# The order of VectorE, ScalarE, GpSimd and the transfers from the scheduler's other model

## The chip, the cores and the metric

The kernel runs on one core of a Trainium2 chip. The metric is device time in microseconds (us), from the start of the program on the core to its end. A core has five engines that run their own instruction queues side by side: TensorE (PE, matrix products), VectorE (DVE), ScalarE (ACT), GpSimd (POOL) and SyncE (SP, which here only issues transfers). An instruction starts when its engine has done the ones before it in its queue and when the operands and buffers that it waits for are ready. The order within a queue is fixed when the program is built.

## The reference

One layer of a hybrid diffusion block, on 512 latent tokens (x) and 256 context tokens (ctx), 2048 wide, all in float32. The core of it:

```python
mod = silu(c) @ w_ada + b_ada
shift, scale, gate = split(mod, 3)             # and the same for ctx, from c_ctx
h  = rms_norm(x, norm_w) * (1 + scale) + shift
hc = rms_norm(ctx, norm_w) * (1 + scale_c) + shift_c
qkv_g, z_g, gates, q_a, k_a, v_a, z_a = split_proj(h @ w_in)       # hc likewise

q, k, v = silu(centred_conv(qkv_g, conv_w))    # 5 taps; q and k are then l2-normed per head
beta = sigmoid(gates[0]); g = -exp(a_log) * softplus(gates[1] + dt_bias)
# 8 heads, two directions, chunks of 64 tokens, first ctx, then latent:
#   v_new = u - w @ s;  o = (q * exp(g)) @ s + intra @ v_new
#   s     = s * exp(g_last) + (k * exp(g_last - g)).T @ v_new
gdn = rms_norm(o_forward + o_backward) * silu(z_g)

attn = softmax(rope(norm(q_a)) @ rope(norm(k_a)).T / sqrt(128)) @ v_a * silu(z_a)   # 8 heads, 2 kv heads
y = concat(gdn, attn) @ w_out
out = rms_norm(x + gate * y, final_norm_w)
```

## The kernel before

The float32 products are made of three passes: each operand is split into a high part (`whi`, `hhL`) and a low part (`wlo`, `hL`), and PE adds high by high, high by low and low by high (L146 to L148 `mm3`, L164 `one`). For each weight piece SP loads the raw tile (`wraw`), ACT casts the high part (L129), and DVE or POOL subtracts the low part (L130); three buffers each go round.

The stages, in time:

- **Start and first projection** (0 to 158 us). Six tiles of 1 MB (`xs`, L296) bring ctx and x; `turn` transposes them on PE. `ada` multiplies c by w_ada, eight groups of four tiles (`wada0_0` is group 0, tile 0; L352 loads, L355 multiplies). From a group's sums (L364) `make_h` builds h for two slices of 128 channels (`hhL` L399, `hL` L401), and `project` (L422) adds their share of the k, q and v columns of the first two heads (`klat`, `qlat`, `vlat`). `first_weights` (L381, L138) loads those columns (`wraw_w0`, `w0r`), L484 the gate columns (`wg`), L503 to L505 constants (`ctri`, `adt`).
- **Gates and the first head** (158 to 215 us). `gates(0, 1)` evaluates the gate formula of head 0 and `gates(1, 8)` that of heads 1 to 7, a chain of 16 small instructions on DVE each (L530 to L540, 128x12 and 128x84). PE sums them up along the tokens (`gcp` L547, L551), DVE copies `gcum` (L552) and `gts` (L564), and two transfers bring the sums back spread over partitions (`growd` L565, then `gr` L631, in the profile `grh`). `conv` (L204) makes the convolution of k, q and v of a head: ACT the first product (L217), DVE the other four taps (L221), ACT an exponential (L224, L225), DVE the last product into `kq`, `kc`, `vv` (L237). `gdn_prep(h)` transposes q and k on PE (`t1`, `t2`, `t3`, L640 to L653), builds the decay matrix in `gr` (L681, L684 on DVE, the exponential L686 on ACT), multiplies (`gq` L693, `IB`, `gr` L240, L702, L709), and inverts. Zero fills (L229) of `ktok`, `IB` and `UU` are ACT's.
- **Scan** (215 to 850 us). `gdn_scan(h)` takes eight heads in turn, twelve steps each. A step is a chain over three engines: `ks` (PE, L852 to L857), `rh` (DVE, L866), `ts` (PE, L875), `vs` and `vn` (ACT, L879, L882), `tsh` (PE, L886), `sth` (DVE, L892); POOL scales the old state (`sdh`, L240). Between these PE runs projections of later heads as filler; meanwhile DVE and ACT prepare the next head.
- **Attention** (850 to 1113 us), eight heads with the z projections as filler.
- **Output projection and end** (1113 to 1303 us). `out_block` (L1497) multiplies by w_out in four blocks of 512 columns; in the first, `merged` (L1486) splits the sixteen input tiles on the way (`mh` on ACT L1491, `ml` on DVE L1492). Each block's `epilogue` (L1522) adds x (`yx`, loaded at L1535) and squares; the last block keeps its weights (`rawl`, L1546). Then the norm and the stores.

**What sets the order.** The code is traced under a `TileContext`. When the context closes, its scheduler orders each engine's queue, among instructions whose inputs it takes to be ready, by the order in the code, moved forward by `tc.high_priority(offset=...)` (so `first_of_all`, offset 2500, round `rh`, `vs` and `sth` of the scan and round the gates of head 0). Two stretches are exempt (`tc.manual_schedule`): there an engine's queue is the order in which the code is written. For PE that is all from L283 to the end of attention; for ACT, DVE and POOL it is the attention. What the scheduler orders is therefore ACT, DVE and POOL outside attention, SP everywhere, and PE in the output projection.

## Time and profile before

| | us |
|---|---|
| median of the runs (lowest 1305.47, highest 1527.16) | 1306.19 |
| the profiled execution | 1304.42 |
| its span | 1302.6 |
| PE busy | 1250.4 |
| DVE busy | 842.5 |
| ACT busy | 583.4 |
| POOL busy | 141.9 |

The profiled execution is one run of the program; its span is the time between the first and the last instruction that the profiler recorded, 1.8 us less than the time of that execution. A row of a timeline gives start and duration in us, engine, line, operation, output and inputs; in brackets, how long the engine had stood idle before it and what ended that. "DVE rh L866" there means that the engine waited for the instruction of L866 on DVE which writes `rh`.

### The profile page before, as it was taken

The numbers are of one execution on the slowest core, as the hardware profiler recorded it, in microseconds if no ns is written. First come the engines' busy times: TensorE is split into PE (matmuls) and PEld (weight loads), VectorE is DVE, ScalarE is ACT, GpSimd is POOL, SyncE is SP. The second block draws the span as 40 slices with busy tenths as digits, with TensorE's granted clock in tenths as the row PEclk, the third lists the DMA queues.
The fourth block names the chain that finished last, engine by engine and source line by source line (L and its number), as shares of the span: only waits on it lengthen the run. The fifth ranks groups of instructions, "written<-read, shape, count | busy, mean of one in ns | idle before, by whom it ended". The sixth has DMA issues, their size and how long they took to land. (4 is left out here: it accounts for less than half of the span.)

```text
span 1302.6 us, 24348 instructions
## 1 busy us (share of the span) xinstructions
PE 1250.4 (96%) x9226; PEld 1018.4 (78%) x9226; DVE 842.5 (65%) x1893; ACT 583.4 (45%) x1464; POOL 141.9 (11%) x206
## 2 busy tenths in 40 slices
PE   6799999999999999999999999999999999999997
PEld 4466688888888888888888877787888888788885
DVE  5444596686867678675776646537888887555432
ACT  4222363455545454544545444535555444434211
POOL 1323100111111111111111001100000000000000
PEclk9999999999999999999999999999999999999998
DMA  9999424231332313222132443356443443475302
GB/s 354 316 326 347 133 67 107 60 67 55 74 72 62 78 47 83 67 69 57 54 83 75 106 131 110 99 164 214 149 129 114 123 140 102 161 244 190 93 33 97
DMA packets 227000, 164.53 MB, mean 126 GB/s; under 512 B 62210, under 2 KB 198491, under 8 KB 225859
## 3 DMA queue, kind: packets, MB, share of 16 engines
q1 hardware_dynamic: 226586, 162.87, 42.9%
q8 instruction: 73, 1.20, 0.4%
q14 instruction: 44, 0.36, 0.1%
q10 hardware_dynamic: 297, 0.11, 0.0%
HBM read 148.85 MB, written 14.08 MB: 125 GB/s over the span
## 5 line engine op out<-in xcount | busy, mean ns | idle before, releaser
L240 POOL TENSOR_TENSOR sdh<-sth,egl 128x256 f32<-128x256 f32 x80 | 56.9, 711 | 446.6 <-DVE sth L892 344.8
L871 ACT ACTIVATE oqh<-ksh,egsw 64x128 f32<-64x128 f32 x128 | 46.3, 362 | 92.7 <-DVE rh L866 86.4
L866 DVE SCALAR_TENSOR_TENSOR rh<-ksh,negeg,vtokh 64x128 f32<-64x128 f32 x176 | 61.2, 348 | 31.1 <-PE ksh L854 24.5
L146 PE MATMUL po<-whi_wo,mh 128*128 128x512 f32 x192 | 76.2, 397 | 0.0
L148 PE MATMUL po<-whi_wo,ml 128*128 128x512 f32 x192 | 76.1, 396 | 0.0
L147 PE MATMUL po<-wlo_wo,mh 128*128 128x512 f32 x192 | 76.1, 396 | 0.0
L1361 PE MATMUL zl<-hhL,whi_z 128*128 128x512 f32 x176 | 74.0, 421 | 0.0
L1361 PE MATMUL zl<-hhL,wlo_z 128*128 128x512 f32 x176 | 69.8, 396 | 0.0
L1361 PE MATMUL zl<-hL,whi_z 128*128 128x512 f32 x176 | 69.6, 395 | 0.0
L130 DVE TENSOR_TENSOR wlo_wo<-wraw_wo,whi_wo 128x512 fp32r<-128x512 f32 x48 | 33.0, 690 | 55.5 <-ACT whi_wo L129 55.3
L886 PE MATMUL tsh<-vsh,ktok 128*128 128x128 f32 x352 | 56.6, 283 | 6.7 <-ACT vnh L882 3.5
L886 PEld LDWEIGHTS tsh<-vsh,ktok 128*128 128x128 f32 x352 | 47.4, 190 | 16.0 <-ACT vnh L882 7.9
L129 ACT CAST whi_wo<-wraw_wo 128x512 fp32r<-128x512 f32 x48 | 29.6, 620 | 67.3 <-PE po L148 56.8
L892 DVE TENSOR_TENSOR sth<-sdh,tsh 128x256 f32<-128x256 f32 x80 | 33.6, 420 | 27.4 <-PE tsh L886 19.2
L879 ACT ACTIVATE vsh<-tsh,cch 128x128 f32<-128x128 f32 x88 | 32.2, 366 | 38.4 <-PE tsh L875 37.1
L164 PE MATMUL vl<-hhL,wlo_v 128*128 128x512 f32 x112 | 46.3, 413 | 0.0
L164 PE MATMUL vl<-hhL,whi_v 128*128 128x512 f32 x112 | 46.2, 413 | 0.0
L164 PE MATMUL vl<-hL,whi_v 128*128 128x512 f32 x112 | 45.8, 409 | 0.0
L1402 DVE SCALAR_TENSOR_TENSOR gacc<-graw,scol,gacc 128x512 f32<-128x512 f32 x60 | 44.9, 748 | 1.0
L950 ACT CAST pth<-pt 128x512 fp32r<-128x512 f32 x48 | 26.8, 585 | 40.7 <-PE pt L1289 40.7
L146 PEld LDWEIGHTS po<-whi_wo,mh 128*128 128x128 f32 x192 | 36.2, 188 | 9.5 <-ACT whi_wo L129 0.8
L148 PEld LDWEIGHTS po<-whi_wo,ml 128*128 128x128 f32 x192 | 36.2, 189 | 8.7
(540 smaller groups left out, 3890.2 us busy)
## 6 DMA issues: line engine op xcount, KB each, us to landing
wada<-in_w_ada SPq DMA_DIRECT2D x64, 512.0 KB, 8.6
graw<-in_w_ada SPq DMA_DIRECT2D x64, 256.0 KB, 3.1
wraw_wo<-in_w_out SPq DMA_DIRECT2D x48, 256.0 KB, 3.3
wraw_z<-in_w_in SPq DMA_DIRECT2D x44, 256.0 KB, 3.1
wraw_v<-in_w_in SPq DMA_DIRECT2D x28, 256.0 KB, 2.9
wraw_k<-in_w_in SPq DMA_DIRECT2D x24, 256.0 KB, 2.9
wraw_q<-in_w_in SPq DMA_DIRECT2D x24, 256.0 KB, 2.8
xs<-in_x SPq DMA_DIRECT2D x4, 1024.0 KB, 5.4
```

What stands on the lines that cost most here:

```text
L130: (lo_eng or G).tensor_tensor(out=lo, in0=raw, in1=hi, op=ALU.subtract)
L146: T.matmul(out, lhsT=lh, rhs=rh, start=start, stop=False, skip_group_check=True)
L147: T.matmul(out, lhsT=lh, rhs=rl, start=False, stop=False, skip_group_check=True)
L148: T.matmul(out, lhsT=ll, rhs=rh, start=False, stop=stop, skip_group_check=True)
L164: T.matmul(out, lhsT=lw, rhs=rt[m], start=k == 0 and n == 0, stop=k == KT - 1 and n == 2, skip_group_check=True)
L240: eng.tensor_tensor(out=out, in0=x, in1=y, op=ALU.mult)
L866: V.scalar_tensor_tensor(out=r[rows], in0=ks[rows, d], scalar=gsc["negeg"][rows, gcol:gcol + 1], in1=vtok[rows, p], op0=ALU.mult, op1=ALU.add)
L871: S.activation(oq[rows, v, p - 2], ks[rows, d], AF.Copy, scale=gsc["egsw"][rows, gcol:gcol + 1])
L886: T.matmul(ts[:, d], lhsT=ktok[:, p, half], rhs=vs, start=True, stop=True, skip_group_check=True)
L892: V.tensor_tensor(out=sn, in0=sd, in1=ts[:, 0:2], op=ALU.add)
L1361: T.matmul(pl, lhsT=lw, rhs=rt, start=k == 0 and m == 0, stop=k == KT - 1 and m == 2, skip_group_check=True)
L1402: V.scalar_tensor_tensor(out=acc, in0=raw, scalar=scol[:, k:k + 1], in1=acc, op0=ALU.mult, op1=ALU.add)
```

## The change

The `TileContext` is told to schedule with its other model. Without the argument it orders by priority with a simple model of readiness; with it, it follows a simulated time line of the engines and picks, for each engine, from what that time line has ready. The instructions are the same ones; PE up to the output projection and the other engines in the attention keep their order.

```diff
@@ -1586,7 +1586,7 @@
         arrays[f"in_{name}"] = arr
         aps[name] = nc.dram_tensor(f"in_{name}", arr.shape, mybir.dt.from_np(arr.dtype), kind="ExternalInput").ap()
     aps["out"] = nc.dram_tensor("out_y", (1, SEQ, D), F32, kind="ExternalOutput").ap()
-    with tile.TileContext(nc) as tc:
+    with tile.TileContext(nc, schedule_with_timeline_sim=True) as tc:
         build(tc, aps)
     r = run_bass_kernel_spmd(nc, [arrays], core_ids=[0])
     return r.results[0]["out_y"]
```

The order changes in hundreds of places; three are shown.

SP, right behind the six loads of `xs`, before (`wada0_0` to `wada0_3` are the first group of w_ada, two transfers each; `wraw_w0_k` and `w0rk` the first projection's weights of slice k; `wg` the gate columns):

```order
L352 DMA wada0_0_372<-in_w_ada 128x4x256 x2
L352 DMA wada0_1_379<-in_w_ada 128x4x256 x2
L352 DMA wada0_2_426<-in_w_ada 128x4x256 x2
L352 DMA wada0_3_433<-in_w_ada 128x4x256 x2
L138 DMA wraw_w0_0_451<-in_w_in 128x2x256
L381 DMA w0r0_457<-in_w_in 128x128
L138 DMA wraw_w0_1_463<-in_w_in 128x2x256
L381 DMA w0r1_469<-in_w_in 128x128
L484 DMA wg_153<-in_w_in 128x16x32
L138 DMA wraw_w0_2_499<-in_w_in 128x2x256
L381 DMA w0r2_505<-in_w_in 128x128
```

And now, from `wraw_w0_2` on; ahead of it stand, in the same sequence as before, `wraw_w0_0`, `w0r0`, `wraw_w0_1`, `w0r1` and `wg` (`ctri` and `adt` are constants of the gates, `nd2` two areas in memory that are cleared from the zeroed `UU0`):

```order
L138 DMA wraw_w0_2_499<-in_w_in 128x2x256
L352 DMA wada0_0_372<-in_w_ada 128x4x256 x2
L381 DMA w0r2_505<-in_w_in 128x128
L503 DMA ctri_110<-in_ctri 128x512
L504 DMA adt_158<-in_a_log 128x16
L505 DMA adt_158<-in_dt_bias 128x16
L352 DMA wada0_1_379<-in_w_ada 128x4x256 x2
L1047 DMA nd20_1634<-UU0_105 48x1024
L1047 DMA nd21_1635<-UU0_105 48x1024
L352 DMA wada0_2_426<-in_w_ada 128x4x256 x2
L138 DMA wraw_w0_3_551<-in_w_in 128x2x256
L352 DMA wada0_3_433<-in_w_ada 128x4x256 x2
```

The first group of w_ada moved behind the weights of three slices, the gate columns, the constants and the two clearings; its last tile also behind the weight of a fourth.

DVE, at the convolution of q of head 0, before (`cacc_q0` are the four taps, `kq0` q's product, `ug` and `gg` the gate formula; 128x12 is head 0, 128x84 heads 1 to 7):

```order
L221 SCALAR_TENSOR_TENSOR cacc_q0_1601<-craw2_1554,cvT_78,cacc_q0_1601 128x512
L130 TENSOR_TENSOR wlo_q0a_0_1836<-wraw_q0a_0_1833,whi_q0a_0_1835 128x512
L221 SCALAR_TENSOR_TENSOR cacc_q0_1601<-craw2_1554,cvT_78,cacc_q0_1601 128x512
L552 COPY gcum_84<-gcp_0_1743 128x12
L221 SCALAR_TENSOR_TENSOR cacc_q0_1601<-craw2_1554,cvT_78,cacc_q0_1601 128x512
L559 TENSOR_SCALAR negeg_85<-negeg_85 128x12
L534 TENSOR_SCALAR ug_112<-w_g_115 128x84
L221 SCALAR_TENSOR_TENSOR cacc_q0_1601<-craw2_1554,cvT_78,cacc_q0_1601 128x512
L564 COPY gts__117<-gtr_0_1767 12x128
L130 TENSOR_TENSOR wlo_q0a_1_1880<-wraw_q0a_1_1877,whi_q0a_1_1879 128x512
L237 SCALAR_TENSOR_TENSOR kq0_1583<-craw2_1554,cacc_q0_1601 128x4x64 x2
L536 SCALAR_TENSOR_TENSOR ug_112<-ug_112,w_g_115 128x84 x5
```

And now (`grh0` is the decay matrix of head 0, which comes from the `gr` load):

```order
L564 COPY gts__117<-gtr_0_1767 12x128
L237 SCALAR_TENSOR_TENSOR kq0_1583<-craw1_1553,cacc_k0_1585 128x4x64 x2
L130 TENSOR_TENSOR wlo_q0a_1_1880<-wraw_q0a_1_1877,whi_q0a_1_1879 128x512
L237 SCALAR_TENSOR_TENSOR kc0_1584<-craw1_1553,cacc_k0_1585 128x2x64 x2
L221 SCALAR_TENSOR_TENSOR cacc_q0_1601<-craw2_1554,cvT_78,cacc_q0_1601 128x512 x2
L681 TENSOR_TENSOR grh0_1785<-grh0_1785,gcum_84 128x768
L221 SCALAR_TENSOR_TENSOR cacc_q0_1601<-craw2_1554,cvT_78,cacc_q0_1601 128x512
L684 TENSOR_TENSOR grh0_1785<-grh0_1785,cmain_75 128x384 x2
L221 SCALAR_TENSOR_TENSOR cacc_q0_1601<-craw2_1554,cvT_78,cacc_q0_1601 128x512
L237 SCALAR_TENSOR_TENSOR kq0_1583<-craw2_1554,cacc_q0_1601 128x4x64 x2
```

`L681` and `L684` moved in between the taps. The 128x84 instructions, here in part before and gone now, moved ahead of the taps of k, one behind each of 128x12; these rows stand there now, just before the first tap of k (`cacc_k0`):

```order
L538 TENSOR_SCALAR ug_112<-ug_112 128x12
L538 TENSOR_SCALAR ug_112<-ug_112 128x84
L539 SCALAR_TENSOR_TENSOR zg_111<-zg_111,ug_112 128x12
L539 SCALAR_TENSOR_TENSOR zg_111<-zg_111,ug_112 128x84
L540 SCALAR_TENSOR_TENSOR gg__116<-zg_111,ag_113 128x12
L540 SCALAR_TENSOR_TENSOR gg__116<-zg_111,ag_113 128x84
L221 SCALAR_TENSOR_TENSOR cacc_k0_1585<-craw1_1553,cvT_78,cacc_k0_1585 128x512
L221 SCALAR_TENSOR_TENSOR cacc_k0_1585<-craw1_1553,cvT_78,cacc_k0_1585 128x256
```

Each instruction of head 0's chain is now followed by the same one for seven heads, and the taps of k follow both; before, they stood one by one between the 128x12 rows.

DVE, in the scan of head 1 while head 3's k is convolved and head 2 is prepared, before (`sth1_2` is the state after step 2 of head 1, `rh1_3` the first product of step 3):

```order
L130 TENSOR_TENSOR wlo_q3_2_3781<-wraw_q3_2_3778,whi_q3_2_3780 128x512
L221 SCALAR_TENSOR_TENSOR cacc_k3_3627<-craw2_1554,cvT_78,cacc_k3_3627 128x512
L221 SCALAR_TENSOR_TENSOR cacc_k3_3627<-craw2_1554,cvT_78,cacc_k3_3627 128x256
L221 SCALAR_TENSOR_TENSOR cacc_k3_3627<-craw2_1554,cvT_78,cacc_k3_3627 128x512
L892 TENSOR_TENSOR sth1_2_3687<-sdh1_2_3611,tsh1_2_3651 128x256
L221 SCALAR_TENSOR_TENSOR cacc_k3_3627<-craw2_1554,cvT_78,cacc_k3_3627 128x512
L221 SCALAR_TENSOR_TENSOR cacc_k3_3627<-craw2_1554,cvT_78,cacc_k3_3627 128x256
L221 SCALAR_TENSOR_TENSOR cacc_k3_3627<-craw2_1554,cvT_78,cacc_k3_3627 128x512
L866 SCALAR_TENSOR_TENSOR rh1_3_3701<-ksh1_3483,negeg_85,vtokh1_2803 64x128 x2
```

And now:

```order
L221 SCALAR_TENSOR_TENSOR cacc_k3_3627<-craw2_1554,cvT_78,cacc_k3_3627 128x512
L221 SCALAR_TENSOR_TENSOR cacc_k3_3627<-craw2_1554,cvT_78,cacc_k3_3627 128x256
L240 TENSOR_TENSOR IB0_1638<-gqh2_3661,grh2_3500 64x4x64 x4
L221 SCALAR_TENSOR_TENSOR cacc_k3_3627<-craw2_1554,cvT_78,cacc_k3_3627 128x512
L221 SCALAR_TENSOR_TENSOR cacc_k3_3627<-craw2_1554,cvT_78,cacc_k3_3627 128x256
L892 TENSOR_TENSOR sth1_2_3687<-sdh1_2_3611,tsh1_2_3651 128x256
L702 TENSOR_TENSOR grh2_3500<-grh2_3500,cch2_3601 128x768
L130 TENSOR_TENSOR wlo_q3_3_3813<-wraw_q3_3_3810,whi_q3_3_3812 128x512
L221 SCALAR_TENSOR_TENSOR cacc_k3_3627<-craw2_1554,cvT_78,cacc_k3_3627 128x512
L221 SCALAR_TENSOR_TENSOR cacc_k3_3627<-craw2_1554,cvT_78,cacc_k3_3627 128x256
L866 SCALAR_TENSOR_TENSOR rh1_3_3701<-ksh1_3483,negeg_85,vtokh1_2803 64x128 x2
```

The four `IB0` products moved ahead of `sth1_2`, and `L702` and a weight's low part in between `sth1_2` and `rh1_3`.

In the output projection's first block ACT and DVE now do the casts and subtractions of all sixteen input tiles (L1491, L1492) before the split of the fourth weight, where before these were mixed; PE starts each slice from the fourth on with its four matmuls of L146; and SP issues 15 of the 16 loads of x (L1535) ahead of the tenth weight, where before they were mixed with the weights behind it.

## The prediction

> **What bounds the kernel now.** I read the page's table of engines first:
>
> ```profile
> span 1302.6 us, 24348 instructions
> PE 1250.4 (96%) x9226; PEld 1018.4 (78%) x9226; DVE 842.5 (65%) x1893; ACT 583.4 (45%) x1464; POOL 141.9 (11%) x206
> ```
>
> TensorE (PE) is busy for 1250.4 of 1302.6 us. No other engine is over 65%, so a new order of the others is worth only what it does to the 52.2 us in which PE stands still. Up to the output projection PE's own order is written out by hand and stays as it is, so PE cannot step around a late operand. The waits of PE say what those 52 us are:
>
> ```profile
> PE xt L314 <- DMA xs<-in_ctx: 6.4, 1, 6.4
> PE ada L355 <- DMA wada<-in_w_ada: 5.1, 5, 1.9
> PE klat L422 <- ACT hhL L399: 3.5, 1, 3.5
> PE tsh L886 <- ACT vnh L882: 3.5, 6, 1.0
> PE tsh L875 <- DVE rh L866: 3.3, 7, 0.7
> PE tsh L886 <- ACT vsh L879: 3.0, 5, 0.9
> PE kvl L164 <- DVE wlo_kv L130: 2.1, 1, 2.1
> PE kvl L164 <- DVE craw L201: 2.1, 1, 2.1
> ```
>
> (Total us, times, longest.) Two kinds: loads at the start, and many short waits for VectorE (DVE) and ScalarE (ACT). The table by stages shows where the slack is thin. Its columns are stretch, length, busy us of PE, of weight loads, DVE, ACT and POOL, granted clock, DMA share, GB/s:
>
> ```profile
> 22.40:38.80 16.40, 9.05 (x56) 4.17 (x56) 8.04 (x22) 3.75 (x11) 4.42 (x6) 0.90 0.99 281
> 38.80:64.00 25.20, 23.06 (x138) 14.28 (x139) 10.64 (x19) 6.16 (x14) 6.13 (x6) 0.93 1.09 348
> 158.00:165.00 7.00, 4.93 (x17) 3.62 (x16) 6.00 (x20) 6.62 (x11) 0.00 (x0) 0.78 0.16 37
> 178.00:188.00 10.00, 10.00 (x65) 8.21 (x64) 9.77 (x29) 9.38 (x33) 0.69 (x1) 1.00 0.35 106
> 215.00:850.00 635.00, 620.70 (x5833) 521.53 (x5832) 433.56 (x1089) 314.49 (x890) 90.11 (x131) 1.00 0.31 77
> 1105.00:1282.00 177.00, 177.00 (x761) 142.43 (x760) 82.05 (x132) 58.29 (x110) 1.12 (x2) 1.00 0.42 140
> ```
>
> Up to 38.8 us the transfers set the pace (share 0.99 while PE is busy 9.05 of 16.4 us). Between 178 and 188 us PE, DVE and ACT are all full: a DVE instruction put forward there is paid by PE. In the scan (215 to 850) PE idles 635.0 - 620.7 = 14.3 us. In the output projection it does not idle at all.
>
> **The change, part by part.** The sum starts from the profiled execution, 1304.4 us (span 1302.6); it is 1.8 below the median of the three runs, 1306.2.
>
> *Start: +4.3.* The first projection waits for h, h for the modulation, and that for the last tile of the first w_ada group (wada0_3):
>
> ```profile
> 32.78 1.07 PE L355 MATMUL ada<-wada,cs 128*32 128x512 f32 x8 [0.82 <-DMA wada<-in_w_ada]
> 38.80 0.66 PE L422 MATMUL klat<-hhL,whi_w 128*128 128x512 f32 x1 [3.49 <-ACT hhL L399]
> PE ada L355 <- DMA wada<-in_w_ada: 1.9, 2, 1.7
> ```
>
> SP now issues ahead of wada0_3 what stood behind it: four wraw_w (128x2x256 f32, 256 KB each), three w0r (128x128, 64 each), wg (128x16x32, 256), ctri (128x512, 256) and two nd2 (48x1024, 192 each): 2112 KB, 2.16 MB. At the 348 GB/s of the next stretch that is 6.2 us (7.7 at the 281 of the stretch itself). The 6.0 us from the arrival at 32.8 to klat at 38.8 stay, so klat comes 6.2 later. What was put forward need not come later, and from 38.8 on, where PE is nearly full, the loads are ahead: the 1.9 us that PE waits there for later w_ada tiles (last row) go. Bounds +2 (if part of the stretch is not held by transfers after all) to +7.7 (the lower rate, and the later waits stay).
>
> *Gates and the first head's prep, 158 to 200 us: +9.4.* Now:
>
> ```profile
> 160.77 0.97 ACT L217 ACTIVATE cacc_k<-craw,cvT 128x770 f32<-128x770 f32 x1
> 161.79 2.87 ACT L229 ACTIVATE ktok<-cmain 128x1536 f32<-128x1536 f32 x2
> 164.53 2.01 ACT L229 ACTIVATE IB<-cmain 128x1024 f32<-128x1024 f32 x2
> 167.76 1.50 ACT L229 ACTIVATE UU<-cmain 128x1536 f32<-128x1536 f32 x1
> 177.74 0.66 PE L640 MATMUL t1h<-cmain,kq 128*128 128x128 f32 x4 [0.26 <-DVE kq L237]
> L536 DVE SCALAR_TENSOR_TENSOR ug<-ug,w_g 128x84 f32<-128x84 f32 x7 | 1.7, 245 | 0.1
> 177.85 1.15 SPq L631 DMA_DIRECT2D grh<-growd  x2
> 183.82 0.96 DVE L681 TENSOR_TENSOR grh<-grh,gcum 128x768 f32<-128x768 f32 x1
> 186.14 1.01 DVE L684 TENSOR_TENSOR grh<-grh,cmain 128x384 f32<-128x384 f32 x2
> DMA to landing us min/median/max: 3.9/3.9/3.9
> ```
>
> PE's transposes of head 0's q and k (t1h) wait for kq even now, by 0.26 us, so kq is on the path. Three things come ahead of it. On ACT, all five zero fills (2.87 + 2.01 + 1.50 = 6.4 us) stand before the convolution's first product (0.97). On DVE the gate formula of heads 1 to 7 (128x84: sixteen instructions, fifteen near 0.24 and a reciprocal, some 4.2 us) is woven into head 0's before the convolution's first sum. Each alone starts that sum at about 168.3 instead of 161.8. And L681 and L684 stand between the four sums of q's convolution, though L681 waits for the gr load, which lands at 177.9 + 3.9 = 181.8. From there: L681 to 182.7, third sum (0.7) to 183.4, L684 to 184.4, fourth sum to 185.1. On ACT the exponential of gr (768 columns, about 0.8 between the fill of 1024 at 1.0 and a cast of 512 at 0.62) then precedes that of q (0.6): from 184.4 to 185.9, and kq's product (0.4) makes it 186.4. t1h moves from 177.7 to 186.4: +8.7. Behind t1h on PE's queue is everything else. Next, PE's gq product waits for the last square of t2, now behind a cast (0.62, as in the projection below) and a convolution product (0.97): +1.6. DVE has then done early what it did later, so the 2.1 us wait for wlo_kv goes.
>
> A stall also costs clock:
>
> ```profile
> 162.22 0.63 PE L164 MATMUL kvl<-hhL,whi_kv 128*128 128x512 f32 x1
> 164.36 0.63 PE L164 MATMUL kvl<-hhL,wlo_kv 128*128 128x512 f32 x1
> ```
>
> After the present wait of 2.1 us at 160.6, six such matmuls (162.22 to 164.36) come one each 0.43 us, where the output projection's 761 come one each 0.23 (177.0 us), and the granted clock of the stretch is 0.78: 6 x 0.20 = 1.2 us, which I add once for the longer stall. [...]
>
> 8.7 + 1.6 + 1.2 - 2.1 = 9.4. Bounds: +5 (if gr lands earlier and only L681 and L684, 2 us, plus the later start count) to +13.
>
> *Scan, 215 to 850: +8.* A step runs ks (PE), rh (DVE), ts (PE), vs (ACT), tsh (PE), sth (DVE), with PE's filler matmuls between. An example, head 1:
>
> ```profile
> 333.97 0.42 DVE L892 TENSOR_TENSOR sth<-sdh,tsh 128x256 f32<-128x256 f32 x1
> 334.31 2.17 DVE L221 SCALAR_TENSOR_TENSOR cacc_k<-craw,cvT,cacc_k 128x512 f32<-128x512 f32 x3
> 336.39 0.71 DVE L866 SCALAR_TENSOR_TENSOR rh<-ksh,negeg,vtokh 64x128 f32<-64x128 f32 x2
> 339.44 0.85 DVE L240 TENSOR_TENSOR IB<-gqh,grh 64x256 f32<-64x256 f32 x2
> 341.91 0.95 DVE L702 TENSOR_TENSOR grh<-grh,cch 128x768 f32<-128x768 f32 x1
> 337.84 0.49 PE L875 MATMUL tsh<-rh,UU 128*128 128x128 f32 x2
> ```
>
> The four IB products (two take 0.85, 1.5 in all) and one more sum of 256 columns (three, two of 512 wide, take 2.17; this one 0.5) now stand before sth: it starts at 336.1 instead of 334.0. L702 (0.95), wlo (0.7) and two sums (1.1) then stand before rh, where now three sums do: it ends at about 339.8 instead of 337.1. It had 337.84 - 337.10 = 0.7 of slack, so PE loses 2.0 here. In the new order I find such a place, by the same reading 0.4 to 2.7 in size, in every head from 1 to 7. One of 1.8 for each of seven heads is 12.6. Other instructions stand earlier than now, and a third of the 14.3 us of present idle may go: -4.8. Net +8. Bounds: -7 (half the present idle goes and the late places are covered by PE having been delayed elsewhere) to +17.
>
> *Attention: 0.* DVE, ACT and POOL are fixed by hand there; only neighbouring loads swap. ±1.
>
> *Output projection: +2.2.*
>
> ```profile
> 1114.08 3.21 ACT L1491 CAST mh<-M 128x512 fp32r<-128x512 f32 x6
> 1122.83 0.62 ACT L129 CAST whi_wo<-wraw_wo 128x512 fp32r<-128x512 f32 x1
> 1118.53 2.48 DVE L1492 TENSOR_TENSOR ml<-M,mh 128x512 fp32r<-128x512 f32 x4
> ```
>
> All fifteen mh casts (six take 3.21, 0.54 each) and ml subtractions (four take 2.48, 0.62 each) now precede the split of the fourth weight. ACT reaches that cast at 1117.3 + 9 x 0.54 = 1122.1, in time: PE leaves the third weight at 1122.83, when the cast that reuses its buffer starts. DVE ends its ml row at about 1125.4 and the fourth weight's low part at 1126.0. PE does the block's four whi matmuls first, as now ordered (0.9 us), and wants it at 1123.8: +2.2. Fifteen yx loads (256 KB each, 3.93 MB, 11.3 us at 348 GB/s) now stand before the tenth weight; from about 1130.5 on they and it land by 1142.5, its cast ends at 1143.1, and PE, 2.2 us late, wants it at 1143.4: just hidden. Bounds 0 (DVE's row runs denser) to +6 (the loads start 4 us later).
>
> Sum: 1304.4 + 4.3 + 9.4 + 8 + 2.2 = 1328.3; plus the 1.8 to the median, **1330 us**.
>
> **Rivals.** *A: the forecast.* Its parts vary to about 1320 to 1342. *B: the losses cancel.* Only the start holds (+4.3); at the gates +5 and the scan's gains and losses even out: 1306.2 + 9 = 1315. For it: once PE is 9 us late at t1h, DVE is ahead, and the scan's first head meets it with slack. Against it: slack gained is used up at the next place where PE waits. *C: the scan pays in full.* +4.3 + 13 + 17 + 6: 1346. For it: the scan is a serial chain, and PE's fixed order makes each late step final. *D, the other side: faster.* The new order follows a time line, so a step's operands come as they are wanted. If it removes two thirds of the scan's 14.3 us (-9.5), the two waits of 2.1 at kvl, and the gates' stall is hidden, then 1306.2 + 4.3 - 9.5 - 4.2 = 1297. It decides if L681 does not in fact hold kq. To be faster by 2% it would have to take 26 of the 52 us of idle, of which 6.4 are the wait for the first load; the waits that an order of the others can shorten, from klat on, are 17.5 us of the list above (3.5 + 3.5 + 3.3 + 3.0 + 2.1 + 2.1). That the order does nothing at all is ruled out before 40 us, where the transfers themselves move.
>
> **How the numbers follow.** A measurement here tells about 2% (26 us) from no change: slower means over 1332.3, faster below 1280.1. A has 0.50, B 0.22, C 0.20, D 0.05, and 0.03 are left for what I have not seen. A's range 1320 to 1342 is cut by 1332.3 a little above its middle: 0.28 same, 0.22 slower. B is same, C slower, D 0.04 same and 0.01 faster; of the rest 0.02 faster, 0.01 slower. Faster 0.03, same 0.54, slower 0.43. The range runs from 1310 (B's lower part; D is left out) to 1347 (C's middle).
>
> **What would show it.** Start: klat near 45 instead of 38.8, and no later PE wait for wada. Gates: t1h about 9 us later against the matmuls before it, waiting for kq, with L681 idle for the gr load just before. Scan: PE idle between the first ts and the attention above 14.3 us by about 8, released by rh, sth, vs. Output projection: one or two waits of a microsecond or two on wlo_wo or whi_wo. I am wrong if PE idle in the scan falls below 14 us, if t1h waits under 3 us, or if klat starts before 42.

## The result: 1357 us, slower by 3.9%, and the profile after

| | before | after |
|---|---|---|
| median of the runs, us | 1306.65 (4 runs) | 1357.41 (1354.21 to 1358.74, 4 runs) |
| ratio to before, 95% interval | | 1.0388 (1.0362 to 1.0414) |
| span of the profiled execution, us | 1302.6 | 1356.6 |

One of before's four runs took 1527.16 us, far above the others, and the ratio leaves it out. The forecast was 1330 us with a range up to 1347, so slower by more than 2% was held possible (0.43), but the size was missed. Of the page of the changed kernel, the table of engines:

```profile
span 1356.6 us, 24351 instructions
PE 1262.0 (93%) x9226; PEld 1026.2 (76%) x9226; DVE 838.9 (62%) x1893; ACT 583.5 (43%) x1464; POOL 142.5 (11%) x206
```

The other engines do the same work in nearly the same time (838.9 us against 842.5 on DVE, the largest difference). PE stands still for 94.6 us instead of 52.2, and its busy time grew by 11.6 us although it runs the same matmuls. PE's larger waits now, without those of the attention (total us, times, longest):

```profile
PE tsh L875 <- DVE rh L866: 11.1, 17, 2.1
PE t1h L640 <- DVE kq L237: 9.5, 1, 9.5
PE tsh L875 <- DVE UU L821: 7.2, 6, 2.4
PE xt L314 <- DMA xs<-in_ctx: 6.1, 1, 6.1
PE ada L355 <- DMA wada<-in_w_ada: 5.7, 3, 4.3
PE po L146 <- ACT whi_wo L129: 5.0, 3, 2.2
PE ksh L857 <- DVE sth L892: 4.4, 3, 1.8
PE rp L333 <- DVE sg L274: 3.9, 1, 3.9
PE ksh L852 <- DVE sth L892: 3.8, 7, 0.9
PE tsh L886 <- ACT vsh L879: 2.5, 3, 0.9
PE tsh L886 <- ACT vnh L882: 2.5, 4, 1.0
PE po L147 <- DVE wlo_wo L130: 2.4, 2, 2.1
PE ksh L857 <- DVE sth L890: 2.4, 2, 2.1
```

In the scan the waits for DVE (`rh`, `UU`, `sth`) grew from 6.5 us to 28.9; those for ACT (`vs`, `vn`) shrank from 6.5 to 5.0. `t1h` waited 0.3 us in before; the two `po` rows are new.

PE's order is the same in both kernels up to the output projection, so each matmul of the one can be set against the same matmul of the other. How much later it starts, counted from the start of its span, is its lag; the growth of the lag over a stage is what the stage costs. The stage edges are the 158, 215, 850 and 1112 us of before; the output projection gets the rest up to the end of the span.

```
lag gained, us          start  gates   scan  attention  output   all
forecast                  4.3    9.4    8       0         2.2   23.9
changed kernel            4.8   11.0   25.3     0.5      12.2   54.0
```

The scan and the output projection hold the miss. Of the 54.0 us, 11.6 are longer busy time of PE: 2.4 at the gates, 4.1 in the scan and 4.8 in the output projection. The last section tells where it comes from.

### The profile page after: what moved, and what is told of

Same layout as the page of the kernel before. It is cut to its first block, busy times and chain, and to the rows that moved or that the text cites. A ratio compares the mean times of both kernels' runs of the same rounds, so it can differ in the third digit from the quotient of the medians.

```text
span 1356.6 us, 24351 instructions
## 1 busy us (share of the span) xinstructions
PE 1262.0 (93%) x9226; PEld 1026.2 (76%) x9226; DVE 838.9 (62%) x1893; ACT 583.5 (43%) x1464; POOL 142.5 (11%) x206
## 5 line engine op out<-in xcount | busy, mean ns | idle before, releaser
L146 PE MATMUL po<-whi_wo,mh 128*128 128x512 f32 x192 | 65.1, 402 | 5.0 <-ACT whi_wo L129 5.0
L146 PEld LDWEIGHTS po<-whi_wo,mh 128*128 128x128 f32 x192 | 36.6, 192 | 16.1 <-ACT whi_wo L129 7.4
L875 PE MATMUL tsh<-rh,UU 128*128 128x128 f32 x176 | 36.8, 291 | 11.2 <-DVE rh L866 11.1
L147 PEld LDWEIGHTS po<-wlo_wo,mh 128*128 128x128 f32 x192 | 36.8, 192 | 12.6 <-DVE wlo_wo L130 3.8
L164 PE MATMUL vl<-hL,whi_v 128*128 128x512 f32 x112 | 45.8, 409 | 0.0
```

The lines of the kernel that those rows point to most:

```text
L146: T.matmul(out, lhsT=lh, rhs=rh, start=start, stop=False, skip_group_check=True)
L147: T.matmul(out, lhsT=lh, rhs=rl, start=False, stop=False, skip_group_check=True)
L164: T.matmul(out, lhsT=lw, rhs=rt[m], start=k == 0 and n == 0, stop=k == KT - 1 and n == 2, skip_group_check=True)
L875: T.matmul(ts[:, 2], lhsT=UU[:, w], rhs=r, start=True, stop=True, skip_group_check=True)
```

## The experiments

All kernels below run the same instructions as the two kernels. Only the order of the queues differs: behind the trace, edges that carry no semaphore tie each instruction to the next one wanted on its engine.

```diff
+def keep_order(nc, tc):
+    for names in ORDER:        # one list per engine
+        for a, b in zip(names, names[1:]):
+            tc.add_manual_dep(nc.get_inst_by_name(b), a, NO_SYNC, reason="order")
...
     with tile.TileContext(nc, schedule_with_timeline_sim=True) as tc:
         build(tc, aps)
+        keep_order(nc, tc)
```

So each edit is told by the rows that change place. Times are medians of 4 runs (11 in the last one) beside runs of before on the same chip; before's medians in the four sets were 1306.4 to 1307.8 us. The split by stages is from one profiled execution of each. Twelve kernels here share the new order of the start, and it cost them 4.8 to 8.0 us; the new order of the gates cost 8.6 to 11.0 in the eleven that have it, that of the scan 22.6 to 27.6 in nine. So a stage's figure is good to 2 or 3 us and a whole time to some 3.

### Which stage pays

```diff
 all queues of the new order, but of one stage the rows in before's order:
+u_start: 0 to 158 us   u_gates: 158 to 215   u_scan: 215 to 850   u_out: from 1113 (PE's too)
 and the reverse:
+alone_scan: before's order everywhere, the scan's rows in the new order
```

> The new order everywhere, except that up to the end of the first projection (158 us) ACT, DVE, POOL and SP have the order of before. Theory 1 (each stage's order costs what PE loses in that stage, and nothing is handed on): the time of the changed kernel, 1357.4, less the 4.9 us that the two traces differ by at the end of this stage, about 1352.5. Theory 2 (a late start makes the later stages lose, since their loads and their DVE work are then out of step): more comes back, 1345 or less.

Measured: 1350.53 us, ratio 1.0327 (1.0304 to 1.0350).

> The new order everywhere, except that from 158 to 215 us (gates and first head) the queues have the order of before. Theory 1: less the 11.1 us that PE falls behind in this stage, about 1346.3, and PE's wait for kq at t1h falls from 9.5 to under 1 us. Theory 2 (the stall at t1h is what puts the scan out of step): the scan's 26 us come back in part too, 1335 or less.

Measured: 1351.13 us, ratio 1.0333 (1.0312 to 1.0355).

> The new order everywhere, except that in the scan (215 to 850 us) the queues have the order of before. Theory 1 (the scan's own order costs it): less 26, about 1331, and PE's waits for rh, sth and UU in the scan fall from 28.9 to about 6.5 us. Theory 2 (the scan loses because it starts late and out of step): little comes back, 1350 or more.

Measured: 1333.34 us, ratio 1.0203 (1.0179 to 1.0226).

> The new order everywhere, except that in the output projection (from 1113 us) all queues, PE's too, have the order of before. Theory 1: less the 12 us that PE falls behind there, about 1345.4, and no PE wait for whi_wo or wlo_wo. Rival: the end is set by loads that are late for other reasons (they were issued late in the attention), and under 4 us come back, 1353 or more.

Measured: 1348.92 us, ratio 1.0314 (1.0291 to 1.0337).

> Order of before everywhere but in the scan (215 to 850 us of before), where VectorE, ScalarE, GpSimd and the transfers have the new order. Theory P (the scan's loss belongs to its own order): 1306.7 + 24 = 1331 us (1327 to 1334). Theory R (it comes in part from reaching the scan 16 us late, with loads and VectorE in another phase): below 1322 us.

Measured: 1329.88 us, ratio 1.0185 (1.0167 to 1.0203).

```
lag gained, us   start  gates   scan  attention  output   all
u_start           -0.6   10.9   22.7     0.8       9.9    43.7
u_gates            5.8   -0.1   26.5     0.7      11.8    44.7
u_scan             7.3    8.9    2.0     0.5       9.6    28.3
u_out              6.8   10.7   25.0     0.9       0.0    43.4
alone_scan         0.4    1.3   22.6     0.4       0.0    24.7
```

In each of the first four the stage that was undone costs 2 us or less, and the others cost what they cost in the changed kernel, within that spread. Undone one by one they win 6.9, 6.3, 24.1 and 8.5 us, 45.8 of the 50.8 between the two kernels. The scan put alone into before costs 22.6. So each stage pays for its own order, and reaching the scan 16 us late neither causes nor cures its loss, as far as the spread lets one see.

### What holds kq at the gates

```diff
 DVE                                  ACT
   L221 cacc_q0 x2                      L225 craw1, L224 craw1, L217 cacc_q0
-  L681 grh0                          - L686 grh0
   L221 cacc_q0                         L225 craw2
-  L684 grh0 x2                         ...
   L221 cacc_q0                         L657 NTh0 x2
   ...                                + L686 grh0
   L661 skh0, L664 sqh0
+  L681 grh0
   ...
   L662 skh0, L666 sqh0
+  L684 grh0 x2
```

> New order everywhere; only four rows of head 0's prep are put back: on VectorE L681 behind L664 and the two L684 behind L666, on ScalarE the exponential L686 behind the last L657, all behind the convolution sums of q and v that they stood in front of. Theory P (the gr load and these rows hold kq): the wait of t1h for kq falls by L681's wait for the load (2.07), L681 (0.9) and two L684 (0.9), 3.9 us together, from 9.5 to about 5.6; time 1357.4 - 4 = 1353.4 us. Theory S (the zero fills and the gate formula alone set kq, the load is not on the path): t1h waits 9 or more, time 1356 to 1358 us.

Measured: 1356.16 us, ratio 1.0384 (1.0364 to 1.0403). DVE in the changed kernel, then `t1h` of the changed kernel (timeline rows):

```profile
172.78 1.15 DVE L221 SCALAR_TENSOR_TENSOR cacc_k<-craw,cvT,cacc_k 128x512 f32<-128x512 f32 x2 [2.35 <-ACT cacc_k L217]
187.31 0.96 DVE L681 TENSOR_TENSOR grh<-grh,gcum 128x768 f32<-128x768 f32 x1 [2.07 <-DMA grh<-growd]
191.78 1.12 PE L640 MATMUL t1h<-cmain,kq 128*128 128x128 f32 x4 [9.53 <-DVE kq L237]
```

and with the four rows put back:

```profile
187.00 1.11 PE L640 MATMUL t1h<-cmain,kq 128*128 128x128 f32 x4 [5.87 <-DVE kq L237]
```

At its place the edit does what was expected: the wait falls by 3.7 us and the stage costs 5.4 instead of 11.0. The other 5.9 us of wait would be, by the working, what comes ahead of the first tap, the zero fills on ACT and the gate formula on DVE; neither was undone by itself, so this is not shown. The end of this execution came only 2.5 us earlier, and the median only 1.2: in it the scan cost 27.1 and the attention 1.6. PE's busy time makes both: 629.1 us in the scan instead of the changed kernel's 624.9, and 258.2 in the attention instead of 256.8, while it idles no longer than there. So what was lost again behind the gates went into slower matmuls, not into new waits; the last section shows where the clock fell in the traces.

### What the scan's loss is made of

The first theory took the loss for the places of the chain's own rows on DVE: too many others in front of them.

```diff
 DVE in the scan: L866 rh, L890 and L892 sth, L821 UU (296 rows)
-  behind as many of the other rows as the new order puts there
+  behind as many of the other rows as before; the others keep their new order
```

> New order everywhere; only VectorE's rows of the scan chain (L866, L890, L892, and L821 of the next head's prep, 296 of its 1089 rows between 215 and 850 us of before) are put back to the places that they had, that is behind as many other rows as before; the other 793 rows keep their new order among themselves, as do ScalarE, GpSimd and the transfers. Theory P (the loss in the scan is the places of the chain's rows, how many others stand in front of each): the scan falls from 25 us over before to 5 or less, time about 1336 us (1331 to 1341), and the waits of tsh for rh and of ksh for sth fall from 20 us together to some 8. Theory Q (the loss is in what order the others come, so that a row in front of the chain waits for its own input, or in ScalarE's order): the scan keeps more than half of its 25, time 1347 us or more.

Measured: 1368.8 us, ratio 1.0473 (1.0457 to 1.0488); the scan cost 35.4 us. Slower than the change itself: the theory fell as it stood. So I looked at what DVE does just before each row for which PE waits. One such place of the changed kernel, DVE, SP and PE (timeline rows):

```profile
388.29 0.42 DVE L892 TENSOR_TENSOR sth<-sdh,tsh 128x256 f32<-128x256 f32 x1
392.64 0.58 DVE L763 STREAM_TRANSPOSE DTh<-DDh 128x384 f32<-128x384 f32 x1 [3.92 <-DMA DDh<-nd]
393.14 0.67 DVE L866 SCALAR_TENSOR_TENSOR rh<-ksh,negeg,vtokh 64x128 f32<-64x128 f32 x2
389.17 1.84 SPq L758 DMA_DIRECT2D DDh<-nd  x4
389.71 0.39 PE L854 MATMUL ksh<-sth,kq 128*128 128x128 f32 x2
393.96 0.46 PE L875 MATMUL tsh<-rh,UU 128*128 128x128 f32 x2 [2.11 <-DVE rh L866]
```

`rh` could start when `ks` is done, at 390.1. In front of it stands L763, a transpose for the next head, whose four loads SP only issues from 389.17 on. DVE stands at it, with nothing to do, for 3.92 us; `rh` starts at 393.14, and PE loses 2.11. In before the two rows stand the other way round:

```profile
373.58 0.71 DVE L866 SCALAR_TENSOR_TENSOR rh<-ksh,negeg,vtokh 64x128 f32<-64x128 f32 x2
374.32 0.58 DVE L763 STREAM_TRANSPOSE DTh<-DDh 128x384 f32<-128x384 f32 x1
```

and L763 waits for nothing, since the load has landed by then. This is no single case. DVE's waits for transfers in the scan, of the changed kernel:

```profile
DVE DTh L763 <- DMA DDh<-nd: 16.6, 7, 3.9
DVE tmh L738 <- DMA NEh<-ndh: 7.4, 4, 2.5
DVE grh L681 <- DMA grh<-growd: 5.5, 7, 1.9
DVE tabq L240 <- DMA tabq<-in_rope: 2.7, 1, 2.7
DVE IB L240 <- DMA IB<-in_rope: 0.6, 1, 0.6
```

32.8 us; and all there are of before:

```profile
DVE grh L681 <- DMA grh<-growd: 3.0, 3, 1.2
DVE tabq L240 <- DMA tabq<-in_rope: 2.3, 1, 2.3
DVE tmh L738 <- DMA NEh<-ndh: 0.6, 1, 0.6
```

5.9 us. Of PE's nineteen waits of 0.6 us or more for DVE in the new scan, 23.1 us, ten have such a row right ahead of the row that PE waits for (14.4 us); in front of the other nine stand rows whose inputs were ready (8.7 us). The transfers are no slower than before (the median from issue to landing of the `DDh` loads is 2.1 us, before 2.5); their readers have come forward. Set against PE's matmuls, DVE comes to L763 earlier by 1.9 to 12.1 us in seven of the eight heads, while SP issues its loads within some 4 us of the old place. The next kernel moves these rows back:

```diff
 DVE in the scan (137 of 1089 rows; 5 rows L686 on ACT follow), for example:
   L892 sth
-  L763 DTh
   L866 rh x2
+  L763 DTh
```

> New order everywhere; in the scan only the VectorE rows that read what a transfer has just brought (L681 and L684 on gr, L763 and the L732, L738, L740 rows on the two triangular tables, the first products on the rope table) are moved back, to the place among the chain's rows that they had before, or in the rope table's case behind L890; 137 of VectorE's 1089 rows of the scan, and 5 exponentials (L686) on ScalarE. The chain's rows and all others keep the new order. Theory T (VectorE stands at a row whose transfer has not landed, with the chain's ready row queued behind): of the 23.1 us of PE waits of 0.6 us or more for VectorE in the new scan, 14.4 us (ten waits) have such a row right ahead of the releasing row; eight of them, 12.9 us, are moved. VectorE's waits for transfers in the scan fall from 33 us to under 12, the scan from 25 us over before to about 11 (8 to 15), time 1344 us (1340 to 1348). Theory M (VectorE's and ScalarE's new orders fit only each other, and any row that is moved makes new waits of the same size, as when the chain's rows were moved): time 1354 us or more.

Measured: 1349.7 us, ratio 1.0325 (1.0305 to 1.0345). DVE's waits for transfers fall to 4.4 us, and the scan costs 14.4 us instead of 25.3. The stretch of the scan as a whole, the changed kernel, then this one (length, busy us of PE, weight loads, DVE, ACT, POOL, clock, DMA share, GB/s):

```profile
230.90:891.20 660.30, 624.84 (x5833) 523.55 (x5832) 430.75 (x1091) 314.11 (x890) 92.51 (x131) 0.99 0.30 74
```

```profile
231.80:881.10 649.30, 620.57 (x5833) 521.51 (x5832) 435.10 (x1091) 313.32 (x890) 91.18 (x131) 1.00 0.31 75
```

PE idles 28.7 instead of 35.5 us: 6.8 of the 12.9 us of waits that were meant to go are won, the rest comes back at other rows (`vs`, 2.5 us before the edit, now 5.9). But its busy time falls too, from 624.84 to 620.57, which is before's 620.70. The 4.3 us go with a lower clock in the changed kernel, 0.66 and 0.67 over the 5 us behind two waits of 2.11 and 2.12 us; they are told of at the end. The stage thus wins 10.9. The time fell by 7.7 only; in the profiled execution the start was 3.2 us dearer than in the changed kernel's.

On what is left, 14.4 us, two more kernels bear:

```diff
 scan_both: as the last one, and
+  L866, L890, L892, L821 on DVE behind as many other rows as before
 scan_act: the new order, and
+  ACT's rows of the scan in before's order
```

> As the run that moved the transfer rows of the scan, and besides the chain's 296 rows are put behind as many other rows of VectorE as before. Theory T (what is left of the scan's loss, 14.3 us, is rows with ready inputs that stand in front of the chain): the scan falls from 14 us over before to 6 or less, time 1349.7 - 9 = 1341 us (1338 to 1344). Theory M (the chain's places and the other rows' order, on VectorE and ScalarE, are matched, and moving the chain's rows breaks the match, as it did without the transfer rows moved): waits of tsh for vs and vn rise again, time 1349 us or more.

Measured: 1344.63 us, ratio 1.0302 (1.0284 to 1.0320); the scan cost 11.8 us. What PE waits for in it:

```profile
PE tsh L886 <- ACT vsh L879: 7.8, 7, 1.8
PE tsh L875 <- DVE rh L866: 4.2, 7, 1.2
PE tsh L886 <- ACT vnh L882: 4.1, 9, 0.9
PE ksh L852 <- DVE sth L892: 3.3, 4, 1.2
```

> New order everywhere; only ScalarE's order in the scan is that of before. Theory T (the scan's loss is VectorE's): the scan keeps 22 to 28 us, time 1354 to 1360 us. Rival A (ScalarE's order has a part of its own of 5 us or more): time 1351 us or less. Theory M (matched orders): the scan gets slower, above 1361 us.

Measured: 1373.62 us, ratio 1.0519 (1.0503 to 1.0535); the scan cost 40.9 us. In it:

```profile
PE tsh L875 <- DVE rh L866: 13.7, 19, 2.3
PE tsh L886 <- ACT vsh L879: 8.4, 6, 3.1
```

`scan_both` fits neither of its theories; `scan_act` came out as theory M had it. The chain's places are worth 2.6 us, no more than the spread, once the transfer rows are out of the way: the waits for `rh` halve (9.3 to 4.2), those for `vs` and `vn` grow (8.7 to 11.9). And ACT's old order in the new surroundings is worse by 16 us than ACT's new one. So in `scan_chain`, `scan_both` and `scan_act` a queue, or a kind of row, taken from the other schedule brought new waits. Of the scan's 25.3 us, 11 are rows that stand at a transfer and 2.6 the chain's places. The last 12 go when ACT, DVE, POOL and SP all get before's order in the scan (`u_scan`), and no single kind of row could be shown to carry them. That they lie in how the orders of DVE and ACT fit each other is argued, not shown: DVE's old order with ACT's new one was not run, nor POOL or SP alone.

### What the output projection pays for

```diff
 SP (out_yx)                        SP, ACT, DVE (out_rawl)
   L138 wraw_wo0_8                  - L1546, L1547, L1548 of the resident weights
-  L1535 yx x15                       between wo0_11 and wo1_6
   L138 wraw_wo0_9                  + behind as many other rows as before,
+  L1535 yx x2                        from wo1_3 to wo2_1
   L138 wraw_wo0_10
+  L1535 yx x2                      out_both: out_rawl, and the yx loads
   ...                                among the others as in before
```

> New order everywhere; only the 16 loads of yx (L1535) are moved on SP's queue: two behind each of the weights wo0_9 to wo1_0, where the new order has 15 of them in a row before wo0_9. Theory P (the row of yx loads delays the tenth weight): the wait of po for whi_wo near 1186 us goes with its 2.2 us and about 1 to 2 us of slower matmuls behind it, time 1357.4 - 3.5 = 1354 us (1352.5 to 1355.5); the waits near 1210 and 1219 us (1.6 and 1.3) stay, being of the rawl rows. Theory U (the transfers are short of rate there whatever their order): the wait moves to another weight, time 1356.5 to 1358.5 us.

Measured: 1360.92 us, ratio 1.0407 (1.0387 to 1.0427); the output projection cost 12.3 us, as in the changed kernel. The wait near 1186 us went, and those at the weights behind grew from 3.2 to 7.6 us; PE's matmuls were quicker by 2.4 us (183.0 us busy instead of 185.5), which hid this in the total. In the changed kernel there is a second cause for these, on ACT (timeline rows):

```profile
1185.35 0.62 ACT L129 CAST whi_wo<-wraw_wo 128x512 fp32r<-128x512 f32 x1 [9.29 <-DMA wraw_wo<-in_w_out]
1218.18 0.62 ACT L1547 CAST wlh<-rawl 128x512 fp32r<-128x512 f32 x1 [1.23 <-DMA rawl<-in_w_out]
1218.70 0.61 ACT L129 CAST whi_wo<-wraw_wo 128x512 fp32r<-128x512 f32 x1
```

and in ACT's list of waits from 1150 to 1260 us:

```profile
ACT wlh L1547 <- DMA rawl<-in_w_out: 16.5, 10, 2.7
```

It is the scan's mechanism on another engine: the cast of a resident weight, not wanted by PE until the last block, stands at its load, and behind it waits the cast `whi_wo` that PE wants now.

> New order everywhere; in the output projection only the last block's resident weights are put back to the places that they had among the others: their loads (L1546) on SP, their casts (L1547) on ScalarE, their subtractions (L1548) on VectorE. Theory T (ScalarE stands at a cast whose load has not landed, 16.5 us in ten waits, with the cast of whi_wo that PE needs queued behind): PE's waits near 1210, 1219 and 1221 us (1.6, 1.3, 0.3) go, those near 1168 and 1186 us (2.1, 2.2) stay; time 1357.4 - 3.2 - about 1 of slower matmuls behind them = 1353 us (1351 to 1355). Rival U (the loads are short of rate there whatever their order): waits of the same sum elsewhere, time 1356 us or more.

Measured: 1353.55 us, ratio 1.0352 (1.0326 to 1.0377); the output projection cost 6.3 us.

> As the run with the resident weights put back, and the loads of yx (L1535) put back to their places among the weights' loads too. Theory T: of PE's waits in the output projection only the 2.1 us for wlo_wo near 1168 us stays (the fifteen subtractions ahead of it are not moved); time 1357.4 - 5.4 - about 2 of slower matmuls = 1350 us (1348 to 1352), the last 2 us above the run that undid the whole stage. Rival U: no better than 1355 us, since spreading yx alone gave nothing.

Measured: 1352.38 us, ratio 1.0348 (1.0329 to 1.0366); the output projection cost 2.5 us. PE's waits in it, from the end of attention on:

```profile
PE po L147 <- DVE wlo_wo L130: 2.1, 1, 2.1
PE pt L1289 <- DVE ptl L951: 1.4, 1, 1.4
```

The second of these is in before too. So of the 12.2 us the resident weights' rows cost 5.9 and the row of `yx` loads 3.8. The last 2.5 are put down to the fifteen `ml` subtractions, which stand ahead of the fourth weight's split that PE still waits for; they were not moved alone. With the resident weights' rows still in the way, spreading the `yx` loads only moved PE's wait on to these, so alone it won nothing.

### All repairs together, and one for before

```diff
 repair: the new order, and
+  the start in before's order; L681, L684, L686 of head 0 as above;
+  the scan's transfer rows as above; out_both's output projection
 before_fix: before's order, and on DVE
+  L890 sth ahead of the first product on the rope table (L240 tabq)
+  L130 wlo_kv1_0 ahead of the four L718 of head 0
```

> All repairs in one kernel: the start in before's order, head 0's gr rows moved back, the scan's transfer rows moved back, the yx loads and the resident weights of the output projection at before's places. If the parts add: start 0, gates +5.5, scan +14.3, attention +1, output projection +2.4, so 1306.5 + 23 = 1330 us (1326 to 1334). If what is won in a stage is given back in the next (the gr rows' 5.2 us were, by 2.6, when done alone): 1336 us or more.

Measured: 1331.47 us, ratio 1.0191 (1.0176 to 1.0207). By stages -0.4, 7.0, 15.8, 2.8 and 2.4 us: the parts add up within 2 us of the expected time, though gates, scan and attention each cost 1.5 to 1.8 more than their part, which is within the spread.

> Order of before, with two rows of VectorE moved: the first product on the rope table, which waits 2.3 us for its load near 781 us, goes behind L890, the copy of the chain for which PE then waits 1.3; and the split wlo_kv for which PE waits 2.1 us near 196 us goes ahead of the four transposes L718 that it stood behind. Theory T: the 1.3 go; the 2.1 go at their place, but PE waits 0.9 us for UU near 239 us already, and up to 2 may come back there: 1303 to 1306 us against 1306.5. Rival: the moved rows make new waits on the chain, 1307 us or more.

Measured: 1306.31 us against 1307.76, ratio 0.9991 (0.9982 to 1.0000): no difference that can be told. The 2.1 us for `wlo_kv` shrink to 0.4 and PE is 2.3 us ahead at 200 us of before, but by 215 the lead is gone: `gcp` (L547) waits 1.5 us for DVE, which it did not before. The 1.3 us at L890 go, and the waits for `rh` grow from 3.3 to 4.9. None of the orders tried is faster than before's.

## Why the prediction was wrong

**Start: right in cause, and near in size partly by luck.** 4.8 us against 4.3. `klat` came 7.5 later (6.2 was the term), and behind it no wait for w_ada is left, as said:

```profile
33.73 1.93 PE L355 MATMUL ada<-wada,cs 128*32 128x512 f32 x8 [4.26 <-DMA wada<-in_w_ada]
41.36 1.07 PE L355 MATMUL ada<-wada,cs 128*32 128x512 f32 x8 [0.76 <-DMA wada<-in_w_ada]
46.26 0.49 PE L422 MATMUL klat<-hhL,whi_w 128*128 128x512 f32 x1 [2.37 <-ACT hhL L399]
```

Three terms were off, and their errors cancelled. The last tile of the first group came at 41.36 instead of 32.78, 8.6 later and not 6.2; from it to `klat` PE took 4.9 us, where 6.0 were to stay; and 2.7 came back behind `klat`, not 1.9. PE's wait of 3.9 us for `sg` (L274) was not foreseen. It lies ahead of the 4.3 us for the w_ada tile, and was not tried apart from the transfers.

**Gates: right.** 11.0 against 9.4, with bounds 5 to 13. `t1h` waited 9.5 for `kq` (8.7 by the working), DVE stood idle for L681's load just before, `gq` waited 1.6 as worked out, and `wlo_kv` is no longer waited for. The slower matmuls (granted clock 0.91 from 173.80 to 230.90, in before 0.97 from 158 to 215) cost 2.4 where 1.2 was charged. One reason given is confirmed: taking the gr rows away shortens the wait by 3.7 us.

**Scan: the step that failed.** Its +8 came from "One of 1.8 for each of seven heads is 12.6" and "a third of the 14.3 us of present idle may go"; the stage cost 25.3. The places that the working named do cost. At the example, PE now waits 2.0 us in two parts, as worked out:

```profile
355.89 0.48 PE L857 MATMUL ksh<-sth,kc 128*128 128x256 f32 x1 [1.28 <-DVE sth L892]
359.56 0.35 PE L875 MATMUL tsh<-rh,UU 128*128 128x128 f32 x1 [0.71 <-DVE rh L866]
```

What the working did not count is in its method: it charged each row in front of the chain with its own duration, and read off the order only rows with ready inputs. A row that stands at a transfer costs the time until that lands: 3.92 us at the L763 above, whose own duration is 0.58. At the gates the same prediction had charged just this for L681, from the load's landing; in the scan it looked neither for L681 nor for L763, L738 and the rope table, whose waits rose from 5.9 to 32.8 us and whose share of the loss, with the slower matmuls behind the longest waits, was 11 us. The rows with ready inputs, charged 12.6 us, stand in front of nine of PE's waits, 8.7 us in all. Nor was a third of the present idle won back: the waits for ACT shrank by 1.5 us. The last 12 us, which no single kind of row carries, were not seen in any form, and their cause stays open.

**Attention: right**, 0.5 against 0.

**Output projection: a term missed and one mis-read.** The wait of 2.1 us for the fourth weight's low part came as worked out (2.2). The tenth weight was called "just hidden"; SP's own row shows why it was not:

```profile
1169.20 10.40 SPq L1535 DMA_DIRECT2D yx<-in_x  x15
```

The working had these loads and the tenth weight on chip 12.0 us after the first was issued, at 348 GB/s. They took from 1169.20 to the cast at 1185.35, 16.2 us; SP came to the tenth weight only at 1180.01. The rate was near the one charged: the transfers moved 334 GB/s in this stretch. But that is 5.4 MB, and the sixteen loads are 4.2; the sum left out the others, such as the three weights that SP had issued from 1167.62 on. PE, 2.1 us late by then, waited 2.2 more. The resident weights' rows on ACT, 5.9 us, were not looked at, and no term was put in for slower matmuls behind the waits, part of the 4.8 us by which PE was busy longer here.

**Rivals.** C, that the scan pays in full, had the mechanism of the outcome, the scan as a serial chain under a fixed PE order, and 1346; its terms of 17 and 6 for scan and output projection were still too small by 8 and 6. B and D are refuted: no loss of one stage was made good by another, and L681 does hold `kq`, by 3.7 us of its wait.

## What to carry to other kernels

When a schedule moves rows of an in-order queue, look first for those that read a fresh transfer, and charge them the time until it lands, not their own duration (3.92 and 0.58 us at L763); what is ready behind them, the critical chain above all, waits too (`rh`, ready at 390.1, started at 393.14). Of the listed waits of an idle engine "<- DMA" is the kind to search for, even on an engine that is busy 60% of the time. And rows taken one kind at a time from another schedule won less here than the waits that they removed (6.8 of 12.9 us in the scan), and could lose (10 us with the chain's rows alone, 16 with ACT's): look at the whole stage after each such repair.

## What was not expected of the hardware

PE's busy time in the scan grew behind single waits. Behind the wait of 2.11 us that ended at 393.96, two stretches of the changed kernel and two matmuls in the first:

```profile
393.96:399.00 5.04, 5.04 (x20) 4.31 (x21) 2.26 (x4) 3.51 (x8) 0.61 (x1) 0.66 0.19 52
399.00:404.00 5.00, 5.00 (x118) 4.05 (x117) 4.21 (x9) 1.87 (x5) 0.00 (x0) 1.00 0.08 19
397.20 0.63 PE L164 MATMUL qal1a<-hhL,whi_q1a 128*128 128x512 f32 x1
398.87 0.39 PE L164 MATMUL qal1a<-hL,whi_q1a 128*128 128x512 f32 x1
```

The granted clock is 0.66 over these 5 us, and a matmul of 512 columns takes 0.63 us instead of 0.39; here it sets in about 1.5 us after the wait has ended. The clock record has this as one stretch of 3.41 us at 0.50, from 395.41 on. In the traces of the changed kernel and of before the record holds only 1.00 and 0.50, and within each of the two the stretches at 0.50, ten and four, start a whole number of 3.41 us apart. The changed kernel's scan has a second one, again of 3.41 us, from 825.49 on, at the end of a wait of 2.12 us (to 825.63); before's scan has none. In the 9.5 us wait for `kq`, which ended at 191.78, the clock went to 0.50 at 187.19 and stayed there for 10.24 us; in the output projection it did so twice for 3.41 us, from 1187.30 and from 1221.43 on.

The length of the wait alone does not tell whether one follows. In the changed kernel's scan the clock stayed at 1.00 over the 5 us behind waits of 2.36 us (to 256.68) and 2.17 us (to 580.83). Read in this way behind 32 waits in the scans of six kernels (the changed kernel, scan_dma, scan_act, alone_scan, scan_chain, scan_both), the clock was 0.66 to 0.68 behind eleven, of 1.81 to 3.11 us, and 1.00 behind the other 21, of 1.50 to 2.38 us. What went with the lower clock in the scan is how long PE was busy, by the profile, in the 3.41 us just before. The changed kernel, columns as for the scan above:

```profile
391.99:395.41 3.42, 1.45 (x8) 1.20 (x9) 1.16 (x3) 1.47 (x5) 0.00 (x0) 1.00 0.31 79
395.41:398.82 3.41, 3.41 (x12) 3.01 (x12) 2.26 (x4) 2.09 (x4) 0.61 (x1) 0.50 0.27 72
822.08:825.49 3.41, 1.43 (x7) 0.81 (x5) 2.35 (x7) 0.96 (x3) 0.00 (x0) 1.00 0.46 170
825.49:828.90 3.41, 3.27 (x8) 2.61 (x9) 2.75 (x10) 1.05 (x4) 2.09 (x2) 0.50 0.31 78
```

Divided into steps of 3.41 us in line with the slow stretches, the scans of the changed kernel and of before have 378: the clock was 0.50 after these two, in which PE was busy for 42%, and 1.00 after all the others, in which it was busy for 61% or more. No limit can be read from that, for outside the scans a step with 1.58 us busy was followed by 1.00 (before, from 196.00) and one with 1.81 by 0.50 (the changed kernel, from 1218.02).

The scans of before and of scan_dma, at a clock of 1.00, ran their matmuls in 620.70 and 620.57 us, the changed kernel's, at 0.99, in 624.84. What makes the clock fall is not shown beyond this.
